# A decoder step on one core: one operand's passes on another engine, gate steps queued behind the weights, a prefilled pair of gate tiles, and a larger bank for the sample transposes

## The chip, the core and the metric

The kernel runs on one core of a Trainium2 chip. A core has a matrix engine (TensorE, PE in the profile, with its weight loads as PEld), a vector engine (VectorE, DVE), a scalar engine (ScalarE, ACT), GpSimd (POOL), and SyncE (SP), which here only issues DMA transfers. Each engine works through its own instructions in order. A waiting instruction therefore holds up everything behind it on that engine.

The metric is the device time of one launch, in microseconds (us). The kernel before takes 2475.88 us, the median of three runs from 2475.53 to 2476.44.

## The reference

One inference step of a layer is computed for a prompt of 512 tokens and for 8 samples of 4 tokens each, 544 tokens together. One wide projection feeds two branches, and a gated merge and a layer norm close the step:

```python
u = einsum('btd,dc->btc', x, w_in)          # D = 2048 -> 18952 columns
q_m,k_m,v_m,o_m,z_m, q_a,k_a,v_a,z_a, g_m,g_a, i_pre,f_pre = split(u)
ig, lf = i_pre + b_igate, log_sigmoid(f_pre + b_fgate)      # 4 heads each: "the gates"
h_m, C, n, m = mlstm(q_m, k_m, v_m, ig, lf, C0, n0, m0)     # 4 heads of 512, matrix memory
h_a = sliding_window_attention(q_a, k_a, v_a, sinks)        # 32 heads of 64, window 128
br_m = norm(h_m) * mlstm_norm_w * sigmoid(o_m) * silu(z_m)
br_a = h_a * silu(z_a)
y = sigmoid(g_m) * (br_m @ w_proj_m) + sigmoid(g_a) * (br_a @ w_proj_a)
out = layernorm(ALPHA * x + y @ w_out)
```

Everything is float32. The new states and the last key and value rows are returned too.

## The kernel before

**Precision.** A float32 operand is split in two float32r parts, a high part (a ScalarE cast) and the rest (a VectorE subtraction). A product is three matmuls: high by high, high by low and low by high. `split` (lines 194 to 203) does this to a 128x1024 tile of weights (`wh`, `wl`, two buffers each in pool `wp`), and `hilo` (243 to 245) to anything else.

**Start (lines 290 to 348).** x arrives in five transfers and is transposed on TensorE, 16 column blocks of 128, into PSUM tiles from `sm()`, a pool of four banks. The samples' 32 rows are transposed into one such tile, `pxs`, which lives until the last block. Each block goes through `hilo` into the operand tiles `a11`, `a21` (first half of the contraction) and `xk2` (second half). GpSimd rebuilds a float32 sum of high and low part (line 340) for `s1r` (from `a21`) and `n2r` (from `a11`), and adds them into `n3r` (line 348).

**Two plain products and the gates (lines 375 to 392 and 595 to 614).** The value columns of attention are computed by `gemm`, in two products of 128 columns, `kk` 0 and 1. Before each half of the second one `gates_half` multiplies the eight gate columns. Its weight tiles `wga`, `wgb` are taken from the `wh` and `wl` buffers, cleared by GpSimd (380, 381) and partly filled; the products go to two banks of the other PSUM pool, `bank()`.

**Paired products (lines 624 to 725).** All further columns are computed two blocks at a time by a scheme with seven block products in place of eight. Its x operands are prepared sums: `s1`, `n2`, `n3`, `s4`, made by the generator `x_sums` (553 to 585). `s4` is `n2r` subtracted from one part of `xk2`, plus the other part: GpSimd does both (577, 578), then `hilo` splits the result. The first pair needs `s4` at its sixth step. A pair has seven steps of 24 matmuls; `prepare` makes a step's weights (sums at line 646 or by an adding DMA at 644, then `split`) and is emitted up to three steps ahead with raised priority. Only two `wh`/`wl` buffers exist, so the cast for one step cannot begin before the step two places earlier has been multiplied. Raw weights come in four pieces, `b11`, `b12` (pool `wr`) and `b22`, `b21` (pool `wr2`, three buffers, which also hold the sum `t1` and, at the start, the samples' rows `xs`).

**Background work.** Generators are advanced by `tick` once per step. `gates` (395 to 521) turns the gate products into the decay tables. It computes `fg` (line 413), sends it through a small DMA to another layout (418), takes Abs and Exp on ScalarE (421, 422), a chain of short VectorE instructions (425 to 434), a DMA back (435), a scan (442), and so on.

**Order of instructions.** A planner orders each engine's instructions by priority and by when its own clock thinks that they are ready. `tc.issue_after(ins)` makes instructions of the same engine come after `ins` in that order. In `paired` all of `prepare`'s VectorE instructions are put after the last plain product's weight subtraction (`plain`, lines 702 and 709). `state["load"]` and `state["split"]` hold the latest weight load and the latest weight subtraction.

Of the kernel before, what the change touches and what calls it, by code (L numbers as in the profile page):

```python
# [16 lines left out]
F32R = mybir.dt.float32r  # L17
# [57 lines left out]
def _build(tc, nc, i, o, es):  # L75
# [25 lines left out]
    def nm(s):  # L101
        count[0] += 1
        return f"{s}_{count[0]}"

    def sm():
        return psB.tile([128, 512], F32, tag="sm", name=nm("sm"))
# [4 lines left out]
    def r32(ap):  # L111
        return ap.bitcast(F32)
# [81 lines left out]
    def split(raw, p=None, tags=("wh", "wl"), parts=1):  # L194
        p = p or wp
        wh = p.tile([128, 8, 128], F32R, tag=tags[0], name=nm("wh"))
        wl = p.tile([128, 8, 128], F32R, tag=tags[1], name=nm("wl"))
        n = 8 // parts
        for k in range(0, 8, n):
            A.copy(wh[:, k:k + n], raw[:, k:k + n])  # L200
            state["split"] = V.tensor_tensor(out=wl[:, k:k + n], in0=raw[:, k:k + n], in1=r32(wh[:, k:k + n]),  # L201
                                             op=ALU.subtract)
        return wh, wl
# [39 lines left out]
    def hilo(src, hi, lo, eng=None):  # L243
        A.copy(hi, src)
        (eng or V).tensor_tensor(out=lo, in0=src, in1=r32(hi), op=ALU.subtract)  # L245
# [41 lines left out]
    def two_k(ch):  # L287
        return slice(ch * 2, ch * 2 + 2)
# [23 lines left out]
    state["load"] = xdma  # L312
    with tc.issue_after(xdma.ins):
        raw0.append(load_half(win, VA_ + 128, 0))
    pxs = sm()
    for g in range(8):
        for q in range(2):
            k = g * 2 + q
            pt = sm()
            for t in range(4):  # L320
                PE.transpose(pt[:, t * 128:t * 128 + 128], xt[k][:, t], ident)
            if k == 2:
                for c in range(4):
                    PE.transpose(pxs[:, c * 128:c * 128 + 128], xs[:, c], ident)
            if k < 8:
                hilo(pt[:, 0:HT], a11[0][:, k], a11[1][:, k])
                hilo(pt[:, HT:SEQ], a21[0][:, k, 0:SEQ - HT], a21[1][:, k, 0:SEQ - HT])
            else:
                hilo(pt[:], xk2[0][k // 4 - 2][:, k % 4, 0:SEQ], xk2[1][k // 4 - 2][:, k % 4, 0:SEQ])
                c = (slice(None), k - 8, slice(0, SEQ - HT))  # L330
                state["x_end"] = V.tensor_tensor(out=s1r[c], in0=pt[:, HT:SEQ], in1=s1r[c], op=ALU.subtract)
        if g % 2:
            k4 = slice((g // 2) * 4, (g // 2) * 4 + 4)
            src = pxs[:].rearrange("p (c q t) -> p q c t", c=4, q=4)[:, g // 2]
            if g < 4:
                hilo(src, *(a21[p][:, k4, SEQ - HT:HT] for p in range(2)))
                for t_, (h_, l_) in ((s1r, a21), (n2r, a11)):
                    for ch in (g - 1, g):
                        ks_ = two_k(ch)
                        G.tensor_tensor(out=t_[:, ks_], in0=r32(h_[:, ks_]), in1=r32(l_[:, ks_]), op=ALU.add)  # L340
            else:
                hilo(src, *(xk2[p][g // 2 - 2][:, :, SEQ:T] for p in range(2)))
                c = (slice(None), slice(k4.start - 8, k4.stop - 8), slice(SEQ - HT, HT))
                V.tensor_tensor(out=s1r[c], in0=src, in1=s1r[c], op=ALU.subtract)
        if g == 3:
            for ch in range(4):
                ks_ = two_k(ch)
                G.tensor_tensor(out=n3r[:, ks_], in0=n2r[:, ks_], in1=s1r[:, ks_], op=ALU.add)
# [26 lines left out]
    def gates_half(ps, half):  # L375
        raw = wr.tile([128, 8, 128], F32, tag="raw", name=nm("graw"))
        nc.sync.dma_start(raw[:, :, 0:8], win[:, half * 8:half * 8 + 8, GI:GI + 8])
        wa = wp.tile([128, 8, 128], F32R, tag="wh", name=nm("wga"))
        wb = wp.tile([128, 8, 128], F32R, tag="wl", name=nm("wgb"))
        G.memset(r32(wa[:]), 0.0)  # L380
        G.memset(r32(wb[:]), 0.0)
        for g in range(2):
            src = raw[:, :, g * 4:g * 4 + 4]
            hi = wa[:, :, g * 32:g * 32 + 4]
            A.copy(hi, src)
            A.copy(wb[:, :, g * 32:g * 32 + 4], src)
            V.tensor_tensor(out=wa[:, :, 64 + g * 32:68 + g * 32], in0=src, in1=r32(hi), op=ALU.subtract)
        for kk in range(8):
            k = half * 8 + kk
            for n, (a, b) in enumerate(((wa, xh), (wb, xl))):  # L390
                for f, c, w in EVEN:
                    PE.matmul(ps[f][:, :w], a[:, kk], b(k, c, w),
                              start=(k == 0 and n == 0), stop=(k == 15 and n == 1))

    def gates(ps):
# [22 lines left out]
        nc.sync.dma_start(f7, fg)  # L418
        yield
        yield  # L420
        A.activation(e7, f7, AF.Abs)
        A.activation(e7, e7, AF.Exp, scale=-1.0)
        yield

        V.tensor_scalar(d7, e7, 2.0, None, op0=ALU.add)
        V.reciprocal(d7, d7)
        V.tensor_tensor(out=s7, in0=e7, in1=d7, op=ALU.mult)
        V.tensor_tensor(out=q7, in0=s7, in1=s7, op=ALU.mult)
# [7 lines left out]
        G.memset(rst, 1.0)  # L436
        G.memset(rst[:, 0:SEQ:128], 0.0)
        G.memset(rst[:, SEQ:T:NTS], 0.0)
        yield
        yield  # L440

        V.tensor_tensor_scan(c, rst, lf, 0.0, ALU.mult, ALU.add)
        ap = lf
        V.tensor_tensor(out=ap, in0=ig, in1=c, op=ALU.subtract)
        yield
# [107 lines left out]
    def x_sums():  # L553
        for ch in range(4):
            ks_ = two_k(ch)
            G.tensor_tensor(out=n2r[:, ks_], in0=n2r[:, ks_], in1=s1r[:, ks_], op=ALU.subtract)
            if ch % 2:
                yield
        for name, r_ in (("s1", s1r), ("n3", n3r), ("n2", n2r)):
            h_, l_ = S[name] = quad(act2, name)  # L560
            for ch in range(4):
                ks_ = two_k(ch)
                with tc.issue_after(state["x_end"].ins):
                    if name == "n3":
                        A.activation(h_[:, ks_], r_[:, ks_], AF.Copy, scale=-1.0)
                        V.scalar_tensor_tensor(l_[:, ks_], r_[:, ks_], -1.0, r32(h_[:, ks_]), op0=ALU.mult,
                                               op1=ALU.subtract)
                    else:
                        hilo(r_[:, ks_], h_[:, ks_], l_[:, ks_])
                if ch % 2:  # L570
                    yield

        for ch in range(4):
            ks_ = two_k(ch)
            k0 = (ch * 2) % 4
            h12, l12 = (r32(xk2[p][ch // 2][:, k0:k0 + 2, 0:HT]) for p in range(2))
            G.tensor_tensor(out=n2r[:, ks_], in0=h12, in1=n2r[:, ks_], op=ALU.subtract)
            G.tensor_tensor(out=n2r[:, ks_], in0=n2r[:, ks_], in1=l12, op=ALU.add)
        while not state.get("plain_done"):
            yield  # L580
        s4 = S["s4"] = quad(act, "s4")
        for ch in range(4):
            ks_ = two_k(ch)
            hilo(n2r[:, ks_], s4[0][:, ks_], s4[1][:, ks_])
            yield

# [109 lines left out]

    AHEAD = 400

    def paired(work):

        steps = [(w, n) for w in work for n in range(7)]
        ready, plain = 0, state["split"]
        with tc.issue_after(state["load"].ins):
            load_a(work[0])
            load_b(work[0])
        for at, (w, n) in enumerate(steps):

            while ready < min(at + 3, len(steps)):
                with tc.high_priority(offset=AHEAD), tc.issue_after(plain.ins):
                    prepare(*steps[ready])  # L710
                ready += 1
            p = at // 7 + 1
            if p < len(work):
                if n == 3:
                    load_a(work[p])
                elif n == 4:
                    load_b(work[p])
            if n == 2 and "early" in w:
                w["early"]()
            half_product(w, n)  # L720
            with tc.high_priority(offset=AHEAD):
                gather(w, n)
            if n == 6:
                w["end"](w["O1"], w["O2"])
            tick()
# [879 lines left out]
    def merge_pair(ct):  # L1605

        merges = []

        def early():
            merges.extend(merged(c) for c in (ct, ct + 1))  # L1610

        def end(o1, o2):
            for c, merge, o in zip((ct, ct + 1), merges, (o1, o2)):
                sg = merge([o[:, 0:HT], o[:, HT:T]])
                nc.sync.dma_start(d_y[c], sg[:])
        return dict(wv=wm, x=XM, cA=ct * 128, cB=ct * 128 + 128, scale=1.0, acc=True, end=end, early=early)

    paired([merge_pair(ct) for ct in range(4, 14, 2)])
    state["end"] = None
    esR.close()  # L1620
    tx = pool(esE, "ty", 6)
# [286 lines left out]
```

## Time and profile before

| | us |
|---|---|
| median of three runs | 2475.88 |
| profiled execution | 2477.29 |
| its span, first to last instruction | 2475.4 |
| TensorE busy | 2441.1 (99%) |
| VectorE busy | 1877.4 (76%) |
| ScalarE busy | 1215.2 (49%) |
| GpSimd busy | 531.7 (21%) |

The windows view gives the busy time of each engine in a stretch of the span, with the number of its instructions, the granted TensorE clock (PEclk, 1.00 is full), the busy share of the DMA engines and what they moved. A timeline row gives start, duration, engine, line, operation, output and inputs, shapes and count; in square brackets stand the idle time of the engine ahead of it and what ended it. `SPq` and `POOLq` rows are the issue of transfers. Starts are counted from the beginning of the span.

### The profile page before, as it was taken

Reading aid. Unit: us, or ns where it says so; the run is one execution under the profiler, and the core shown is the slowest. Engines: PE = TensorE matmul, PEld = TensorE weight load, DVE = VectorE, ACT = ScalarE, POOL = GpSimd, SP = SyncE. Lnnn points to the kernel's source line nnn. Section 1 sums busy time; section 2 is a strip of 40 time slices with the busy share of each in tenths; the row PEclk is TensorE's granted clock in tenths of the full one; section 3 lists DMA queues with packets and bytes.
Section 4 is the critical chain, followed back from the end, with each engine's and each line's share of the span. In section 5 each row is a group of like instructions: output and inputs, shape, how many; then the busy total and the mean of one; then the engine's idle time right before and its main releaser. Section 6 shows DMA issues by size and latency. Waiting matters only on the chain.

```text
span 2475.4 us, 48813 instructions
## 1 busy us (share of the span) xinstructions
PE 2441.1 (99%) x19446; PEld 2383.9 (96%) x19446; DVE 1877.4 (76%) x2805; ACT 1215.2 (49%) x1984; POOL 531.7 (21%) x492
## 2 busy tenths in 40 slices
PE   8999999999999999999999999999999999999997
PEld 8999999999999999999999999999999999999997
DVE  6768888888888887778877888887866654766667
ACT  4447667666667665443433444444633333344431
POOL 7113433433433431121011122111000000110111
PEclk9999999999999999999999999999999999999999
DMA  5676666676676655467678667587755546788776
GB/s 159 153 195 170 150 166 152 149 171 150 149 169 154 146 135 150 115 204 235 207 221 250 195 207 231 171 253 237 237 189 177 177 153 212 212 228 252 215 222 190
DMA packets 557435, 464.72 MB, mean 188 GB/s; under 512 B 45592, under 2 KB 454344, under 8 KB 556952
## 3 DMA queue, kind: packets, MB, share of 16 engines
q1 hardware_dynamic: 540312, 402.09, 54.6%
q0 software_dynamic: 15696, 57.15, 12.0%
q8 instruction: 153, 2.51, 0.4%
q10 hardware_dynamic: 1200, 2.36, 0.3%
q14 instruction: 74, 0.61, 0.1%
HBM read 319.06 MB, written 96.31 MB: 168 GB/s over the span
## 4 chain that ended last, share of the span: by engine, by line
PE 89%; DMA 4%; DVE 3%; POOL 1%; issue 1%; ACT 0%; SPq 0%; DVEq 0%; POOLq 0%; ACTq 0%
PE bank L666 45%; PE bank L668 22%; PE bank L210 10%; PE sm L1412 2%; PE bank L1224 1%; PE sm L1444 1%; PE sm L776 1%; PE sm L1457 1%; PE sm L822 1%; DMA tx<-d_y 1%; DMA ty<-d_y 1%; PE sm L1774 1%; DMA raw<-in_w_in 1%; DVE wl L201 1%; PE sm L802 1%
## 5 line engine op out<-in xcount | busy, mean ns | idle before, releaser
L200 ACT CAST wh<-raw 128x1024 fp32r<-128x1024 f32 x632 | 662.1, 1048 | 846.1 <-PE bank L666 682.8
L201 DVE TENSOR_TENSOR wl<-raw,wh 128x1024 fp32r<-128x1024 f32 x632 | 790.7, 1252 | 210.6 <-ACT wh L200 184.2
L666 PE MATMUL bank<-xk,wh 128*128 128x272 f32 x2336 | 322.7, 289 | 0.0
L646 DVE TENSOR_TENSOR raw<-raw,raw 128x1024 f32<-128x1024 f32 x238 | 303.5, 1276 | 7.6 <-DMA raw<-in_w_in 3.0
L666 PEld LDWEIGHTS bank<-xk,wh 128*128 128x128 f32 x2336 | 302.7, 188 | 3.5 <-issue 2.6
L685 POOL TENSOR_TENSOR ev<-p,ev 128x272 f32<-128x272 f32 x82 | 118.0, 1439 | 442.0 <-ACT ev L684 419.4
L666 PE MATMUL bank<-n2h,wh 128*128 128x272 f32 x656 | 171.2, 293 | 2.9 <-ACT wh L200 2.9
L666 PE MATMUL bank<-s1h,wh 128*128 128x272 f32 x656 | 169.8, 292 | 1.8 <-ACT wh L200 1.8
L666 PE MATMUL bank<-n3h,wh 128*128 128x272 f32 x656 | 169.4, 290 | 0.3 <-DVE ev L687 0.3
L668 PE MATMUL bank<-xk,wl 128*128 128x272 f32 x1168 | 169.6, 287 | 0.0
L666 PE MATMUL bank<-n2l,wh 128*128 128x272 f32 x656 | 169.2, 289 | 0.0
L666 PE MATMUL bank<-s1l,wh 128*128 128x272 f32 x656 | 168.0, 288 | 0.0
L666 PE MATMUL bank<-n3l,wh 128*128 128x272 f32 x656 | 167.7, 288 | 0.0
L666 PE MATMUL bank<-s4h,wh 128*128 128x272 f32 x656 | 167.1, 288 | 0.0
L666 PE MATMUL bank<-s4l,wh 128*128 128x272 f32 x656 | 166.8, 287 | 0.0
L668 PEld LDWEIGHTS bank<-xk,wl 128*128 128x128 f32 x1168 | 155.5, 188 | 0.0
L666 PE MATMUL bank<-a11h,wh 128*128 128x272 f32 x584 | 150.4, 289 | 0.3 <-ACT wh L200 0.3
L666 PE MATMUL bank<-a11l,wh 128*128 128x272 f32 x584 | 149.6, 288 | 0.0
L210 PE MATMUL bank<-bh,wl 128*128 128x272 f32 x704 | 148.3, 289 | 0.0
L210 PE MATMUL bank<-bh,wh 128*128 128x272 f32 x704 | 148.0, 289 | 0.0
L210 PE MATMUL bank<-bl,wh 128*128 128x272 f32 x704 | 146.0, 288 | 0.2 <-DVE bl L245 0.2
L644 POOL DMA_DIRECT2D raw<-raw x90 | 78.0, 867 | 277.2 <-DVE ev L693 202.2
(490 smaller groups left out, 5697.0 us busy)
## 6 DMA issues: line engine op xcount, KB each, us to landing
raw<-in_w_in SPq DMA_DIRECT2D x296, 512.0 KB
raw<-raw POOLq DMA_DIRECT2D x90, 512.0 KB, 4.9
C<-in_state_mlstm_C SPq DMA_DIRECT2D x32, 1024.0 KB
out<-C SPq DMA_DIRECT2D x64, 512.0 KB
raw<-in_w_proj_a SPq DMA_DIRECT2D x32, 512.0 KB
raw<-in_w_proj_m SPq DMA_DIRECT2D x32, 512.0 KB
raw<-in_w_out SPq DMA_DIRECT2D x32, 512.0 KB
d_v<-ev SPq DMA_DIRECT2D x16, 272.0 KB
```

The costliest lines, as they stand in the source:

```text
L200: A.copy(wh[:, k:k + n], raw[:, k:k + n])
L201: state["split"] = V.tensor_tensor(out=wl[:, k:k + n], in0=raw[:, k:k + n], in1=r32(wh[:, k:k + n]), op=ALU.subtract)
L210: PE.matmul(ps[f][:, :w], a[:, kk], b(k, c, w), start=(k == 0 and n == 0), stop=(k == 15 and n == 2))
L644: G.dma_start(out=w[out][:], in_=w[b][:], accum_op=ALU.add)
L646: V.tensor_tensor(out=w[out][:], in0=w[a][:], in1=w[b][:], op=ALU.add)
L666: PE.matmul(ps, wh[:, k], x(p, k), start=(first and k == 0 and p == 0), stop=False, skip_group_check=True)
L668: state["end"] = PE.matmul(ps, wl[:, k], x(0, k), start=False, stop=(k == 7), skip_group_check=True)
L685: G.tensor_tensor(out=c22, in0=p1, in1=c11, op=ALU.subtract)
L776: PE.matmul(pp[:, c0 + w0:c0 + 256], qs[a][:, j * 128:j * 128 + 128], kx[:, k0:k0 + 256 - w0], start=(n == 0), stop=(n == 1))
L802: PE.transpose(pt[:, b * 128:b * 128 + 128], s_[:, b, 128:256], ident)
L822: PE.matmul(po[:, b * 128:b * 128 + n], VA[:, b], p_[:, 2 * b:2 * b + n // 128], start=(b == 0 and m == 0), stop=(b == 3 and m == 1), skip ...
L1412: PE.matmul(pp[:, 0:258], a[:, b * 128:b * 128 + 128], b_[:, b, f], start=(b == 0 and n == 0), stop=(b == 3 and n == 2))
```

## The change

Five things are changed.

1. The two passes over `n2r` for `s4` are done by VectorE, not by GpSimd, and stand in the same loop as `s4`'s split, behind the end of the plain products.
2. `gates`' Abs is ordered behind the latest weight cast on ScalarE. Its VectorE chain and its scan are ordered behind the latest weight subtraction. The scan is emitted one tick later.
3. The gate weights have two tiles of their own, from pool `wr2`, cleared once by GpSimd at the start and used for both halves.
4. The samples are transposed into a tile of `bank()`, not of `sm()`.
5. `s1r` is copied from the transposes by ScalarE, eight copies of 240 columns and two of the samples' columns, in place of the GpSimd sums of `a21`. And `prepare` is ordered behind the plain subtraction only in the pairs of `w_proj_m`, not in those of `w_in` and `w_out`.

```diff
-            A.copy(wh[:, k:k + n], raw[:, k:k + n])
+            state["cast"] = A.copy(wh[:, k:k + n], raw[:, k:k + n])
...
-    pxs = sm()
+    gate_w = [wr2.tile([128, 8, 128], F32R, tag="raw2", name=nm("wg")) for _ in range(2)]
+    for t_ in gate_w:
+        G.memset(r32(t_[:]), 0.0)
+    pxs = bank()
...
                 hilo(pt[:, HT:SEQ], a21[0][:, k, 0:SEQ - HT], a21[1][:, k, 0:SEQ - HT])
+                A.copy(s1r[:, k, 0:SEQ - HT], pt[:, HT:SEQ])
...
-                for t_, (h_, l_) in ((s1r, a21), (n2r, a11)):
-                    for ch in (g - 1, g):
-                        ks_ = two_k(ch)
-                        G.tensor_tensor(out=t_[:, ks_], in0=r32(h_[:, ks_]), in1=r32(l_[:, ks_]), op=ALU.add)
+                A.copy(s1r[:, k4, SEQ - HT:HT], src)
+                for ch in (g - 1, g):
+                    ks_ = two_k(ch)
+                    G.tensor_tensor(out=n2r[:, ks_], in0=r32(a11[0][:, ks_]), in1=r32(a11[1][:, ks_]), op=ALU.add)
...
-        wa = wp.tile([128, 8, 128], F32R, tag="wh", name=nm("wga"))
-        wb = wp.tile([128, 8, 128], F32R, tag="wl", name=nm("wgb"))
-        G.memset(r32(wa[:]), 0.0)
-        G.memset(r32(wb[:]), 0.0)
+        wa, wb = gate_w
...
-        A.activation(e7, f7, AF.Abs)
+        with tc.issue_after(state["cast"].ins):
+            A.activation(e7, f7, AF.Abs)
...
-        V.tensor_scalar(d7, e7, 2.0, None, op0=ALU.add)
+        with tc.issue_after(state["split"].ins):
+            V.tensor_scalar(d7, e7, 2.0, None, op0=ALU.add)
...
-        yield
-        yield
-
-        V.tensor_tensor_scan(c, rst, lf, 0.0, ALU.mult, ALU.add)
+        for _ in range(3):
+            yield
+
+        with tc.issue_after(state["split"].ins):
+            V.tensor_tensor_scan(c, rst, lf, 0.0, ALU.mult, ALU.add)
...
+        while not state.get("plain_done"):
+            yield
+        s4 = S["s4"] = quad(act, "s4")
         for ch in range(4):
...
-            G.tensor_tensor(out=n2r[:, ks_], in0=h12, in1=n2r[:, ks_], op=ALU.subtract)
-            G.tensor_tensor(out=n2r[:, ks_], in0=n2r[:, ks_], in1=l12, op=ALU.add)
-        while not state.get("plain_done"):
-            yield
-        s4 = S["s4"] = quad(act, "s4")
-        for ch in range(4):
-            ks_ = two_k(ch)
+            V.tensor_tensor(out=n2r[:, ks_], in0=h12, in1=n2r[:, ks_], op=ALU.subtract)
+            V.tensor_tensor(out=n2r[:, ks_], in0=n2r[:, ks_], in1=l12, op=ALU.add)
             hilo(n2r[:, ks_], s4[0][:, ks_], s4[1][:, ks_])
...
-    def paired(work):
+    def paired(work, plain=None):
...
-        ready, plain = 0, state["split"]
+        ready = 0
...
-                with tc.high_priority(offset=AHEAD), tc.issue_after(plain.ins):
+                with tc.high_priority(offset=AHEAD), tc.issue_after(plain.ins) if plain else ExitStack():
                     prepare(*steps[ready])
...
-    paired([merge_pair(ct) for ct in range(4, 14, 2)])
+    paired([merge_pair(ct) for ct in range(4, 14, 2)], state["split"])
```

More of the change, by code (lines that the diff above doesn't have):

```diff
@@ L571, in x_sums @@
                     yield
-        for ch in range(4):
-            ks_ = two_k(ch)
[L575 to L578, printed above, removed]
         while not state.get("plain_done"):
@@ L583, in x_sums @@
             ks_ = two_k(ch)
+            k0 = (ch * 2) % 4
+            h12, l12 = (r32(xk2[p][ch // 2][:, k0:k0 + 2, 0:HT]) for p in range(2))
+            V.tensor_tensor(out=n2r[:, ks_], in0=h12, in1=n2r[:, ks_], op=ALU.subtract)
+            V.tensor_tensor(out=n2r[:, ks_], in0=n2r[:, ks_], in1=l12, op=ALU.add)
             hilo(n2r[:, ks_], s4[0][:, ks_], s4[1][:, ks_])
```

## The prediction

> **What bounds the kernel now.** I read the page's totals first, then the windows of 50 us over the whole span, then windows of 10 us over the start, and at last each engine's timeline there.
>
> ```profile
> span 2475.4 us, 48813 instructions
> PE 2441.1 (99%) x19446; PEld 2383.9 (96%) x19446; DVE 1877.4 (76%) x2805; ACT 1215.2 (49%) x1984; POOL 531.7 (21%) x492
> ```
>
> TensorE is idle for 2475.4 - 2441.1 = 34.3 us in all. No edit here removes a matmul of the products, so only idle time and slow-clock time can be won. The windows of the first 120 us show where they are.
>
> ```profile
> 0.00:10.00 10.00, 6.69 (x35) 6.70 (x36) 0.68 (x3) 2.25 (x5) 0.83 (x7) 1.00 0.84 238
> 10.00:20.00 10.00, 8.16 (x53) 7.70 (x52) 6.07 (x15) 6.02 (x17) 6.42 (x5) 0.83 1.09 358
> 20.00:30.00 10.00, 8.89 (x75) 8.70 (x74) 8.47 (x17) 6.62 (x17) 10.00 (x9) 1.00 0.36 34
> 30.00:40.00 10.00, 8.43 (x65) 7.85 (x63) 9.30 (x17) 5.81 (x14) 6.33 (x7) 1.00 0.59 154
> 40.00:50.00 10.00, 8.69 (x68) 8.34 (x68) 7.25 (x10) 5.02 (x12) 8.57 (x6) 1.00 0.55 146
> 50.00:60.00 10.00, 9.98 (x80) 9.77 (x80) 9.68 (x8) 4.47 (x9) 10.00 (x6) 1.00 0.20 54
> 60.00:70.00 10.00, 6.28 (x34) 5.73 (x33) 6.94 (x14) 4.88 (x10) 2.97 (x6) 0.69 0.47 106
> 70.00:80.00 10.00, 10.00 (x68) 9.99 (x68) 5.23 (x12) 3.48 (x5) 3.31 (x4) 0.80 0.49 108
> 80.00:90.00 10.00, 10.00 (x82) 10.00 (x82) 10.00 (x17) 3.16 (x3) 0.85 (x1) 1.00 0.63 173
> 90.00:100.00 10.00, 8.53 (x67) 7.97 (x66) 9.85 (x26) 6.28 (x11) 0.00 (x0) 1.00 0.58 144
> 110.00:120.00 10.00, 10.00 (x82) 10.00 (x81) 6.66 (x8) 4.35 (x6) 1.90 (x2) 1.00 0.78 190
> ```
>
> After the length of each stretch come PE, PEld, DVE, ACT and POOL, then the granted clock. The reader should see three things. An undisturbed 10 us hold 82 matmuls. The two windows from 60 to 80 hold 34 + 68 = 102 of 164, which is 62 / 8.2 = 7.6 us lost; 3.7 us of that are idle (10.00 - 6.28) and the other 3.9 us are the clock at 0.69 and 0.80. And VectorE is full from 80 to 100, where TensorE loses another 1.47 us.
>
> The waits of TensorE behind these numbers:
>
> ```profile
> 12.65 0.59 PE L210 MATMUL bank<-a21h,wh 128*128 128x272 f32 x1 [0.48 <-ACT a21h L244]
> 23.09 0.63 PE L321 MATMUL sm<-cc,xr 128*128 128x128 f32 x4 [1.11 <-DVE a21l L245]
> 33.71 0.37 PE L392 MATMUL bank<-a11h,wga 128*128 128x272 f32 x1 [1.19 <-DVE wga L387]
> 39.08 0.40 PE L210 MATMUL sm<-a11h,wh 128*128 128x272 f32 x1 [0.39 <-ACT wh L200]
> 40.74 0.44 PE L530 MATMUL sm<-cc,ev 128*128 128x128 f32 x2 [0.67 <-ACT ev L605]
> 41.93 0.39 PE L210 MATMUL sm<-a11h,wl 128*128 128x272 f32 x1 [0.64 <-DVE wl L201]
> 62.80 0.39 PE L666 MATMUL bank<-s1h,wh 128*128 128x272 f32 x1 [1.78 <-ACT wh L200]
> 67.96 0.59 PE L666 MATMUL bank<-n2h,wh 128*128 128x272 f32 x1 [1.94 <-ACT wh L200]
> 95.73 0.39 PE L666 MATMUL bank<-n2h,wh 128*128 128x272 f32 x1 [1.00 <-ACT wh L200]
> ```
>
> And ScalarE just before the two longest of them:
>
> ```profile
> 57.06 0.65 ACT L244 CAST s4h<-n2r 128x544 fp32r<-128x544 f32 x1 [2.98 <-POOL n2r L578]
> 61.16 0.64 ACT L244 CAST s4h<-n2r 128x544 fp32r<-128x544 f32 x1 [1.14 <-POOL n2r L578]
> 61.71 1.04 ACT L200 CAST wh<-raw 128x1024 fp32r<-128x1024 f32 x1
> 66.50 0.22 ACT L421 ACTIVATE t<-t 128x17 f32<-128x17 f32 x1 [3.06 <-DMA t<-t]
> 66.88 1.03 ACT L200 CAST wh<-raw 128x1024 fp32r<-128x1024 f32 x1
> ```
>
> The weight casts that TensorE waits for are not late by themselves. The one at 61.71 stands behind `s4h` casts that wait for GpSimd's passes, and the one at 66.88 behind the gates' Abs, which waits for the small DMA of `fg`. After 100 us the span holds few such waits, so what is won or lost at the start passes to the end.
>
> **The change part by part.**
>
> *The passes on VectorE and Abs behind a cast (60 to 80 us).* Both causes go. The passes leave GpSimd, so `s4h` waits for VectorE only. `s4`'s tiles take over those of `a21`, free when TensorE has finished the first half of the second plain product at 51.6, before the first pair. When Abs is emitted, two ticks into the first pair, the latest cast emitted is that of step 3, so Abs falls behind the casts of steps 2 and 3 (before, it stood ahead of step 2's). Then its DMA can be 3 us late without a matmul waiting. Queued behind it there are step 4's cast and ScalarE's copies out of PSUM. I take the whole 7.6 us as won; the low end is the 3.7 us of idle time alone, if the clock stays low for another reason.
>
> The price is on VectorE:
>
> ```profile
> 50.15 2.04 DVE L201 TENSOR_TENSOR wl<-raw,wh 128x1024 fp32r<-128x1024 f32 x1 [2.90 <-ACT wh L200]
> 52.12 2.38 DVE L646 TENSOR_TENSOR raw<-raw,raw 128x1024 f32<-128x1024 f32 x1
> 56.26 1.85 DVE L201 TENSOR_TENSOR wl<-raw,wh 128x1024 fp32r<-128x1024 f32 x1
> 58.03 1.88 DVE L245 TENSOR_TENSOR s4l<-n2r,s4h 128x544 fp32r<-128x544 f32 x1
> 61.66 0.71 DVE L245 TENSOR_TENSOR s4l<-n2r,s4h 128x544 fp32r<-128x544 f32 x1 [1.74 <-issue]
> 63.97 1.21 DVE L646 TENSOR_TENSOR raw<-raw,raw 128x1024 f32<-128x1024 f32 x1
> 65.11 1.21 DVE L201 TENSOR_TENSOR wl<-raw,wh 128x1024 fp32r<-128x1024 f32 x1
> L577 POOL TENSOR_TENSOR n2r<-xk,n2r x4: 1363/1860/3047, 45.4 to 53.4; 128x544 f32<-128x544 f32 x4
> ```
>
> Eight passes of 128x544 at 0.71 each are 5.7 us. Against that, the four VectorE instructions beside GpSimd's passes took 2.04 + 2.38 + 1.85 + 1.88 = 8.15, and the same shapes without them 1.21 + 1.21 + 1.21 + 0.71 = 4.34, so 3.8 us come back. Net 1.9 us more work. Its cover is VectorE's idle time from 40 to 80 us, 40 - (7.25 + 9.68 + 6.94 + 5.23) = 10.9 us. If TensorE runs some 8 us sooner, that cover shrinks by as much, and about 10.9 - 8 - 1.9 = 1 us is left before the stretch where VectorE is full. So it is nearly used up. I charge 1.0 us, the size of the wait that VectorE's queue already causes at 95.73; the ends are 0 and the 1.9 us of added work, and a gain of 1.0 if that wait itself goes.
>
> *Gate tiles of their own.* The waits at 39.08 and 41.93 come from the weight buffers: the gate tiles sat in them, so the second plain product's cast and subtraction started late. With buffers free the split can run before 39 us. I take 0.39 + 0.64 = 1.0 us; the wait of 0.67 at 40.74 belongs to copies on ScalarE and may go (high end) or stay. The two clears of 128x1024 move to the beginning, where POOL is busy for 0.83 of 10 us: nothing. The wait at 33.71 (1.19) I do not count. The second gate bank is now the one that `pxs` held, and that comes free only with the last reader:
>
> ```profile
> 35.50 0.28 DVE L344 TENSOR_TENSOR r<-sm,r 128x128 f32<-128x128 f32 x1
> 34.06 1.57 SPq L637 DMA_DIRECT2D raw<-in_w_in  x2
> 41.90 0.37 SPq L187 DMA_DIRECT2D raw<-in_w_in  x1
> ```
>
> GpSimd's earlier finish draws that reader forward, so the ends are a gain of 1.2 and a loss of 1.2.
>
> Another queue is touched. Before, `b22` and `b21` were requested at 34.06. Now two of the three `wr2` buffers hold gate tiles until the gates' last matmul, at about 49 us; `b21` and the sum `t1` wait for them. `b21` is first used three steps into the pair, some 9 us after the plain products end at 57.7, so a request at 49 is early enough: cost 0. If its request stands in SyncE's order ahead of `b11` (41.90), the first weights of the pair queue behind it; this is a rival below.
>
> *`pxs` in a bank and `s1r` from ScalarE (10 to 25 us).* A fourth transpose tile turns over, and GpSimd loses four sums. The wait at 23.09 came from a subtraction queued behind a weight subtraction that GpSimd's sum had stretched:
>
> ```profile
> 20.50 2.13 DVE L201 TENSOR_TENSOR wl<-raw,wh 128x1024 fp32r<-128x1024 f32 x1 [0.51 <-ACT wh L200]
> 11.78 0.36 ACT L244 CAST a21h<-sm 128x240 fp32r<-128x240 f32 x1
> ```
>
> I take the 1.1 us. ScalarE gets eight copies like the 0.36 one and two smaller, some 3.5 us, and has 20 - 6.02 - 6.62 = 7.4 us idle from 10 to 30. A late copy of this kind cost 0.48 at 12.65; I charge 0.5. Ends: 0 and 3.5.
>
> *The rest.* Gates' chain and scan behind splits, one tick later, and `prepare` without its order edge: the subtractions they are ordered against are ready before the other inputs in each case; cost 0, ends a microsecond either way.
>
> *Sum.* 7.6 - 1.0 + 1.0 + 1.1 - 0.5 = 8.2 us. The span becomes 2467.2 and the profiled execution, 1.9 us longer than its span, 2469.1. The median lies 1.4 us under the profiled execution, so 2475.88 - 8.2 = 2467.7.
>
> **The rivals.**
>
> *The clock stays low.* TensorE is idle for only 1.78 and 1.94 us before and in the slow stretch, while the 1.11 and 1.19 us at 23 and 34 are followed by full clock. If something other than these waits slows it, 3.9 us of the sum go: 2471.6. The timing speaks for the waits, because the clock is 1.00 in the window before them and falls after the first.
>
> [...]
>
> *A wait at the new buffers.* SyncE stands at `b21` from about 35 to 49 us, and `b11`, `b12` come some 7 us later than 41.90. TensorE then waits up to 4 us at the start of the first pair, and as at 62.80 the clock may follow (3.9): 2467.7 + 7.9 = 2475.6. For it: before, both loads were requested together at 34.06, ahead of `b11`. Against it: the planner orders a transfer by when its buffer comes free.
>
> *VectorE takes GpSimd's place (slower).* The gates' steps from 79 to 100 us share VectorE with the splits; busy time there is 19.85 of 20. A pair of steps later on that engine by the passes and with less cover would cost TensorE its waits in full. If the passes stand ahead of the splits, 5.7 us of them plus the four `s4l` at 0.71 (2.8) hold back weights, and the 3.9 us of slow clock follow: 12.4 lost where 8.2 and the 1.0 already charged are won, which gives 2479.1. It decides from a VectorE backlog of 5.3 us on (9.2 - 3.9). Against it: split instructions have raised priority, and passes can run before 51 us.
>
> *More is won.* The waits at 33.71, 40.74 and 95.73 go too (1.2 + 0.7 + 1.0), and the two charges (1.5) are not paid: 12.6 us, 2463.3.
>
> **How the numbers follow.** The forecast has 0.52, more won 0.18, the low clock 0.08, the new buffers 0.10, VectorE 0.12. 0.2% is 5 us, about what a measurement of this kernel can tell. Faster by more: 0.52 + 0.18 = 0.70. Within: 0.18 (low clock, buffers). Slower: 0.12. The range goes from 2462 (more won, and another microsecond from the order edges) to 2476 (the buffers' case), which leaves VectorE's case and little of the others outside.
>
> **What would show it.** Right: no `s4h` cast waiting for POOL, no weight cast behind Abs, a clock of 1.00 from 50 to 80 us, the second plain product's cast before 39 us, and the first pair starting 2 us sooner. Wrong: a new TensorE wait for a weight cast or subtraction in the first two pairs, SyncE waiting for TensorE at L637 with L187 behind it, or a clock under 1.00 somewhere between 15 and 80 us.

## The result, and the profile after

| | before | after |
|---|---|---|
| median of six runs, us | 2476.16 (2475.12 to 2478.39) | 2467.02 (2465.84 to 2469.53) |
| profiled execution, us | 2477.29 | 2469.53 |
| its span, us | 2475.4 | 2467.7 |

The ratio is 0.9963, with an interval from 0.995 to 0.9976: 9.1 us less. The page's totals of after:

```profile
span 2467.7 us, 48808 instructions
PE 2436.4 (99%) x19446; PEld 2379.8 (96%) x19446; DVE 1876.5 (76%) x2813; ACT 1216.6 (49%) x1994; POOL 509.8 (21%) x478
```

GpSimd's work falls by 22 us and VectorE's stays the same, although it took over eight passes. The windows of after, columns as before:

```profile
20.00:30.00 10.00, 6.59 (x51) 5.90 (x50) 6.04 (x14) 4.58 (x18) 5.06 (x4) 1.00 0.36 35
30.00:40.00 10.00, 10.00 (x82) 10.00 (x83) 9.70 (x15) 8.69 (x19) 5.78 (x4) 1.00 0.60 160
40.00:50.00 10.00, 10.00 (x82) 10.00 (x82) 10.00 (x18) 4.11 (x8) 0.00 (x0) 1.00 0.54 144
50.00:60.00 10.00, 10.00 (x84) 9.99 (x83) 10.00 (x14) 7.51 (x15) 1.27 (x2) 1.00 0.44 102
60.00:70.00 10.00, 10.00 (x83) 9.99 (x82) 8.91 (x23) 5.06 (x9) 4.17 (x5) 1.00 0.58 119
70.00:80.00 10.00, 10.00 (x82) 10.00 (x81) 7.67 (x12) 3.34 (x4) 1.91 (x3) 1.00 1.00 261
90.00:100.00 10.00, 8.86 (x71) 8.88 (x72) 9.62 (x21) 7.45 (x12) 0.40 (x1) 1.00 0.94 211
110.00:900.00 790.00, 790.00 (x6357) 789.81 (x6356) 647.08 (x951) 516.91 (x953) 273.79 (x210) 1.00 0.66 159
```

From 30 to 80 us TensorE is never idle in this profile, and always at full clock: the waits at 33.71, 39.08, 40.74, 41.93, 62.80 and 67.96 are all gone. But the window from 20 to 30 is worse than before, 6.59 busy where it was 8.89. The last row gives the rate to convert with: 6357 matmuls in 790 us, 8.05 per us.

TensorE's timeline of after shows what the bad window waits for, and the wait near 90:

```profile
25.49 0.40 PE L210 MATMUL bank<-xk,wh 128*128 128x272 f32 x1 [0.60 <-ACT xk L244]
29.89 0.52 PE L210 MATMUL bank<-xk,wh 128*128 128x272 f32 x2 [2.38 <-ACT xk L244]
91.14 0.37 PE L668 MATMUL bank<-n3h,wh 128*128 128x272 f32 x1 [1.32 <-DVE ev L689]
```

ScalarE's timeline of after, ahead of the wait of 2.38 us, and at the passes and Abs:

```profile
24.64 0.22 ACT L369 CAST sel<-cc 128x32 fp32r<-128x32 f32 x1 [2.00 <-DMA cc<-in_consts]
28.78 0.22 ACT L386 CAST wg<-graw 128x32 fp32r<-128x32 f32 x1 [3.12 <-DMA graw<-in_w_in]
29.26 0.57 ACT L244 CAST xk<-sm 128x512 fp32r<-128x512 f32 x1
...
53.04 1.28 ACT L244 CAST s4h<-n2r 128x544 fp32r<-128x544 f32 x2 [1.12 <-DVE n2r L585]
65.65 0.22 ACT L423 ACTIVATE t<-t 128x17 f32<-128x17 f32 x1 [0.79 <-DMA t<-t]
```

The `xk` cast that TensorE waits for at 29.89 stands in ScalarE's queue behind the copies into the gate tiles (lines 386, 387), and these wait 3.12 us for the raw gate columns to arrive. (The wait of 0.60 at 25.49 has another cause: its cast stands behind the copy of a constant, `sel`, that waits for `cc`.) Before, the gate tiles were weight buffers that came free later, so those copies were queued later. With tiles that are cleared at the start nothing else holds them back, and they moved ahead of the casts of x. SyncE's queue says why the columns are late:

```profile
18.94 5.43 SPq L365 DMA_DIRECT2D sinkb<-in_attn_sinks  x1
24.41 0.67 SPq L366 DMA_DIRECT2D sinkc<-in_attn_sinks  x1
25.20 1.13 SPq L381 DMA_DIRECT2D graw<-in_w_in  x2
```

The request of `graw` comes only after one that held the queue for 5.43 us.

**The same kernel before, profiled twice more.** The loss that the prediction was mostly made of, from 60 to 80 us, is not in these two profiles. The first of them:

```profile
30.00:40.00 10.00, 6.60 (x49) 5.78 (x47) 6.94 (x9) 5.61 (x14) 8.66 (x7) 0.93 0.60 161
40.00:50.00 10.00, 8.04 (x51) 8.05 (x52) 6.11 (x12) 3.00 (x7) 5.71 (x4) 0.72 0.54 139
60.00:70.00 10.00, 8.55 (x69) 8.34 (x68) 8.93 (x20) 4.81 (x10) 1.15 (x4) 1.00 0.49 106
```

```profile
41.95 0.60 PE L210 MATMUL sm<-a11h,wl 128*128 128x272 f32 x1 [4.30 <-DVE wl L201]
65.97 0.39 PE L666 MATMUL bank<-n2h,wh 128*128 128x272 f32 x1 [1.45 <-ACT wh L200]
```

```profile
35.86 4.91 DVE L566 SCALAR_TENSOR_TENSOR n3l<-r,n3h 128x544 fp32r<-128x544 f32 x4
40.69 1.21 DVE L201 TENSOR_TENSOR wl<-raw,wh 128x1024 fp32r<-128x1024 f32 x1
```

Here TensorE waits 4.30 us at 42, for the second plain product's weight subtraction. That one stands behind four `n3l` steps which took 4.91 us. And the clock is 0.72 around that wait, while it stays at 1.00 from 60 to 80. The span is the same within 1 us: 2475.5, and 2474.5 in the other. So the kernel before loses its time in one of two forms, and the prediction knew one. The form goes with the first 20 us. The two profiles of the first form (before, and only_passes below) start the first plain product at 11.65 and 12.08 us and have a clock of 0.83 from 10 to 20. The three of the second (with only_gate_order) start it at 10.85 to 11.01 and have 1.00. What makes that difference isn't shown.

**Where the time went, by stretches.** Matmuls that TensorE did in four stretches of the start, from the windows view of every profile (8.05 of them are 1 us; the last two columns are sums):

| kernel | 0 to 30 | 30 to 50 | 50 to 80 | 80 to 110 | 0 to 50 | 50 to 110 |
|---|---|---|---|---|---|---|
| before, as predicted from | 159 | 132 | 177 | 221 | 291 | 398 |
| before_again | 179 | 100 | 224 | 205 | 279 | 429 |
| before_third | 178 | 92 | 227 | 205 | 270 | 432 |
| after | 143 | 162 | 244 | 229 | 305 | 473 |
| after_again | 147 | 153 | 244 | 239 | 300 | 483 |
| undo_passes | 153 | 153 | 217 | 220 | 306 | 437 |
| undo_gate_order | 162 | 163 | 231 | 226 | 325 | 457 |
| undo_tiles | 172 | 125 | 237 | 232 | 297 | 469 |
| undo_start | 163 | 163 | 239 | 210 | 326 | 449 |
| only_passes | 159 | 132 | 219 | 218 | 291 | 437 |
| only_gate_order | 177 | 97 | 239 | 231 | 274 | 470 |
| gates_behind_x | 182 | 162 | 243 | 235 | 344 | 478 |
| sinks_later | 178 | 161 | 244 | 228 | 339 | 472 |

Means of three and two profiles: before 280 and 420, after 302.5 and 478. That is 22.5 / 8.05 = 2.8 us won before 50 us and 58 / 8.05 = 7.2 us behind it, 10 us together, and nearly all of it reaches the end: 9.1 us in the median. Of the 7.2 us, 4.3 lie from 50 to 80 (244 against a mean of 209.3) and 2.9 from 80 to 110 (234 against 210.3).

The first column also holds a difference that is not the kernels': the first plain product starts between 10.76 and 12.17 us, from one execution to the next (12.17 and 11.36 in the two of after).

### The profile page after: what moved, and what is told of

Its sections match the earlier page's. It is cut to its first block, busy times and chain, and to the rows that moved or that the text cites. A ratio compares the mean times of both kernels' runs of the same rounds, so it can differ in the third digit from the quotient of the medians.

```text
span 2467.7 us, 48808 instructions
## 1 busy us (share of the span) xinstructions
PE 2436.4 (99%) x19446; PEld 2379.8 (96%) x19446; DVE 1876.5 (76%) x2813; ACT 1216.6 (49%) x1994; POOL 509.8 (21%) x478
## 4 chain that ended last, share of the span: by engine, by line
PE 92%; DMA 3%; DVE 2%; SPq 1%; issue 1%; ACT 0%; DVEq 0%; POOL 0%; POOLq 0%
PE bank L668 45%; PE bank L670 22%; PE bank L210 10%; PE sm L1414 2%; PE bank L1226 1%; PE sm L1446 1%; PE sm L778 1%; PE sm L1459 1%; PE sm L824 1%; PE sm L210 1%; DMA tx<-d_y 1%; DMA ty<-d_y 1%; PE sm L1776 1%; DMA raw<-in_w_in 1%; PE sm L804 1%
```

## The experiments

**The passes back on GpSimd** (`undo_passes`), all else as in after:

```diff
+        for ch in range(4):
+            ...
+            G.tensor_tensor(out=n2r[:, ks_], in0=h12, in1=n2r[:, ks_], op=ALU.subtract)
+            G.tensor_tensor(out=n2r[:, ks_], in0=n2r[:, ks_], in1=l12, op=ALU.add)
         while not state.get("plain_done"):
             yield
...
-            V.tensor_tensor(out=n2r[:, ks_], in0=h12, in1=n2r[:, ks_], op=ALU.subtract)
-            V.tensor_tensor(out=n2r[:, ks_], in0=n2r[:, ks_], in1=l12, op=ALU.add)
```

> The changed kernel with only the two passes for the fourth operand back on GpSimd, in their old place. Theory (the prediction's first term): the weight cast of the first pair's second step stands again behind fourth-operand casts that wait for GpSimd; TensorE idles 1.5 to 2 us near 60 us, and the granted clock falls below 1.00 for some microseconds behind it. Loss against the changed kernel 1.8 (the wait alone) to 5.7 us (with 3.9 of slow clock): 2469 to 2473. Rival (the passes cost on VectorE what they save on ScalarE): within 1 us of the changed kernel, 2466 to 2468, and VectorE visibly less full from 40 to 60 us. On the clock: if waits cause the slow clock, PEclk is under 1.00 between 60 and 80 us; if it slows for another reason, that does not follow the wait.

Measured: 2474.51 us, ratio 0.999 [0.998, 0.9999]. That is 7.5 us over after, or 6.7 by the two ratios, and more than the expected 2469 to 2473. ScalarE's and TensorE's timelines:

```profile
53.04 0.65 ACT L244 CAST s4h<-n2r 128x544 fp32r<-128x544 f32 x1 [3.06 <-POOL n2r L582]
56.17 0.65 ACT L244 CAST s4h<-n2r 128x544 fp32r<-128x544 f32 x1 [2.48 <-POOL n2r L582]
58.48 0.65 ACT L244 CAST s4h<-n2r 128x544 fp32r<-128x544 f32 x1 [1.66 <-POOL n2r L582]
```

```profile
60.13 0.39 PE L670 MATMUL bank<-s1h,wh 128*128 128x272 f32 x1 [1.48 <-ACT wh L200]
```

The `s4h` casts wait for GpSimd again, and TensorE for a weight cast behind them. Up to 50 us the kernel stands where after stands (306 against 305 and 300); from 50 to 110 it is 41 matmuls short of the mean of after, 5.1 us. The clock, which was expected to fall behind the wait, is 1.00 from 50 to 80 us. The rest of the loss lies later. In this profile there are 5396 matmuls from 1700 to 2380 us, where after has 5418 and 5417; whether that is so in every execution isn't settled.

**The gates' order edges and the later tick taken out** (`undo_gate_order`):

```diff
-        with tc.issue_after(state["cast"].ins):
-            A.activation(e7, f7, AF.Abs)
+        A.activation(e7, f7, AF.Abs)
...
-        with tc.issue_after(state["split"].ins):
-            V.tensor_scalar(d7, e7, 2.0, None, op0=ALU.add)
+        V.tensor_scalar(d7, e7, 2.0, None, op0=ALU.add)
...
-        for _ in range(3):
-            yield
-        with tc.issue_after(state["split"].ins):
-            V.tensor_tensor_scan(c, rst, lf, 0.0, ALU.mult, ALU.add)
+        yield
+        yield
+        V.tensor_tensor_scan(c, rst, lf, 0.0, ALU.mult, ALU.add)
```

> The changed kernel without the order edges on the gates' Abs, VectorE chain and scan, and with the scan one tick sooner, as before. Theory: Abs stands ahead of a weight cast again and waits for its small transfer; TensorE idles up to 1.9 us near 65 us, alone or with a slow clock: 2468 to 2471. Rival (in the changed kernel that transfer is early enough, or Abs falls behind the casts anyway): no TensorE wait there, 2466 to 2468.

Measured: 2469.23 us, 0.9969 [0.9956, 0.9982], 2.2 us over after, with ranges that overlap. The total of matmuls up to 110 us is that of after, but it is made of two parts. The start went better, with a wait of 0.72 us at 27 and not of 2.38, though the edit changes nothing there: in this execution the first plain product started at 10.76 us, in after at 12.17, and the clock from 10 to 20 us was 0.83, not 1.00. From 50 to 110 it lacks 21 matmuls of after's mean, 2.6 us; 13 of them (1.6 us) lie before 80, and behind 80 the two profiles of after differ by 10 themselves. No wait is left near 65, where the prediction put Abs. There is a new one at 78.27, and VectorE's timeline shows what it waits behind:

```profile
78.27 1.27 PE L667 MATMUL bank<-a11h,wl 128*128 128x272 f32 x8 [1.32 <-DVE wl L201]
```

```profile
75.47 1.28 DVE L443 TENSOR_TENSOR_SCAN t<-t,t 4x544 f32<-4x544 f32 x1 [3.61 <-DMA t<-t]
76.68 0.40 DVE L692 SCALAR_TENSOR_TENSOR ev<-bank,ev 128x272 f32<-128x272 f32 x1
77.01 1.20 DVE L201 TENSOR_TENSOR wl<-raw,wh 128x1024 fp32r<-128x1024 f32 x1
```

VectorE stood 3.61 us at the scan, which waited for its small transfer, and the weight subtraction was queued behind it. In after that subtraction stands ahead of the scan, which waits for its transfer there too, but TensorE has no wait near it:

```profile
74.74 1.22 DVE L201 TENSOR_TENSOR wl<-raw,wh 128x1024 fp32r<-128x1024 f32 x1
77.31 1.28 DVE L446 TENSOR_TENSOR_SCAN t<-t,t 4x544 f32<-4x544 f32 x1 [1.35 <-DMA t<-t]
```

So with the passes moved it is the scan's place that pays, not that of Abs. Its edge and its later tick were taken out together, so which of the two is needed stays open.

**The gate tiles back in the weight buffers** (`undo_tiles`):

```diff
-    gate_w = [wr2.tile([128, 8, 128], F32R, tag="raw2", name=nm("wg")) for _ in range(2)]
-    for t_ in gate_w:
-        G.memset(r32(t_[:]), 0.0)
...
-        wa, wb = gate_w
+        wa = wp.tile([128, 8, 128], F32R, tag="wh", name=nm("wga"))
+        wb = wp.tile([128, 8, 128], F32R, tag="wl", name=nm("wgb"))
+        G.memset(r32(wa[:]), 0.0)
+        G.memset(r32(wb[:]), 0.0)
```

> The changed kernel with the gate tiles taken from the weight buffers and cleared for each half, as before. Theory: the second plain product's split waits for the gate products again, TensorE loses about 1 us around 40 us: 2468. Rival (the shared buffers delay the whole hand-over to the pairs, and with it casts near 50 to 60 us): 3 us or more and a wait there, 2470 or above. Second rival (the early gate copies on ScalarE, which in the changed kernel hold the transposes' casts until their transfer lands, near 29 us, go away with the late tiles): TensorE's wait of 2.4 us at 29.9 vanishes and the sum is even, 2465 to 2467.

Measured: 2469.42 us, 0.9969 [0.9957, 0.9982], 2.4 us over after, or 1.5 by the two ratios. The start gets better and the next stretch worse: from 20 to 30 us it does 70 matmuls where after does 51 and 48 (2.5 us), then from 30 to 50 it does 125 against 157.5 (4.0 us). The copies now stand behind more of the x casts. They still wait 1.29 us for `graw`, but TensorE's longest wait for an `xk` cast is 0.27 us, not 2.38. It waits again at 36 to 39, with a clock of 0.91 from 30 to 50:

```profile
38.47 0.44 PE L534 MATMUL sm<-cc,ev 128*128 128x128 f32 x2 [1.70 <-ACT ev L607]
```

So the tiles won 4.0 us and gave 2.5 back, 1.5 net.

**The start as before** (`undo_start`): `pxs` from `sm()`, `s1r` by GpSimd.

```diff
-    pxs = bank()
+    pxs = sm()
...
-                A.copy(s1r[:, k, 0:SEQ - HT], pt[:, HT:SEQ])
...
-                A.copy(s1r[:, k4, SEQ - HT:HT], src)
-                ... (n2r alone by GpSimd)
+                for t_, (h_, l_) in ((s1r, a21), (n2r, a11)):
+                    ...
```

> The changed kernel with the sample transposes in the smaller pool and the float sums of the second half-operand on GpSimd, as before. Theory (1.1 won less 0.5 charged): 2467.6, with the wait of about 1 us at 23 us back. Rival (ScalarE's ten copies are why the changed kernel loses 2.3 us more from 20 to 30 us): that loss goes, 2464 to 2466. Second rival (that loss comes from gate copies waiting for their transfer on ScalarE): the wait near 29 us stays in this kernel too.

Measured: 2469.98 us, 0.9971 [0.9959, 0.9982]. The wait for a transpose tile is back, and the wait for the x cast is shorter than in after, but still there:

```profile
20.69 0.63 PE L324 MATMUL sm<-cc,xr 128*128 128x128 f32 x4 [0.76 <-DVE a21l L245]
27.17 0.52 PE L210 MATMUL bank<-xk,wh 128*128 128x272 f32 x2 [1.40 <-ACT xk L244]
```

That part decides little by itself. Up to 50 us this kernel is ahead of after (326 against 302.5); from 80 to 110 it loses 24 matmuls (210 against 234) to weight casts and subtractions that come late. Why they do there was not pursued.

**The passes alone, in before** (`only_passes`): line 577 and 578 to VectorE, in the loop behind the plain products.

```diff
-            G.tensor_tensor(out=n2r[:, ks_], in0=h12, in1=n2r[:, ks_], op=ALU.subtract)
-            G.tensor_tensor(out=n2r[:, ks_], in0=n2r[:, ks_], in1=l12, op=ALU.add)
...
+            V.tensor_tensor(out=n2r[:, ks_], in0=h12, in1=n2r[:, ks_], op=ALU.subtract)
+            V.tensor_tensor(out=n2r[:, ks_], in0=n2r[:, ks_], in1=l12, op=ALU.add)
```

> The kernel before with only the two passes moved to VectorE. Theory as predicted (two separate causes, passes and Abs): the wait of 1.78 near 62 us goes, the one of 1.94 at Abs stays, and the slow clock stays or shrinks: 2 to 5 us faster than before, 2471 to 2474. Rival (the passes are the whole cause: with them gone the gates' first values and their transfer come early, and Abs no longer waits): both waits and the slow clock go, 7 us or more, 2469 or below. Second rival (without the gate tiles VectorE holds back weights): no gain.

Measured: 2474.35 us, 0.9993 [0.9984, 1.0002]: not clear of the noise, and 4 us at most, while undoing the same edit in after costs 7.5 us. The profile has before's first form, and does 39 matmuls more than that one from 50 to 110 us (437 against 398), so something is won there. VectorE's timeline, and TensorE's wait:

```profile
47.25 2.61 DVE L580 TENSOR_TENSOR n2r<-xk,n2r 128x544 f32<-128x544 f32 x4
49.80 2.61 DVE L581 TENSOR_TENSOR n2r<-n2r,xk 128x544 f32<-128x544 f32 x4
52.34 1.21 DVE L201 TENSOR_TENSOR wl<-raw,wh 128x1024 fp32r<-128x1024 f32 x1
```

```profile
53.60 0.52 PE L210 MATMUL sm<-xk,wl 128*128 128x272 f32 x2 [1.30 <-DVE wl L201]
```

The plain product's last weight subtraction stands behind all eight passes. This is the mechanism of the third rival, VectorE in GpSimd's place, at a price of 1.3 us. It does not act in after, where that subtraction is done by 44.9, before the passes begin:

```profile
43.67 1.21 DVE L201 TENSOR_TENSOR wl<-raw,wh 128x1024 fp32r<-128x1024 f32 x1
47.35 2.61 DVE L584 TENSOR_TENSOR n2r<-xk,n2r 128x544 f32<-128x544 f32 x4
```

Gate tiles of their own are not needed for that. In undo_tiles, without them, the subtraction stands behind all eight passes too, but the passes begin at 41.89 and not at 47.25, and TensorE does not wait for it:

```profile
41.89 0.70 DVE L584 TENSOR_TENSOR n2r<-xk,n2r 128x544 f32<-128x544 f32 x1
48.94 1.21 DVE L201 TENSOR_TENSOR wl<-raw,wh 128x1024 fp32r<-128x1024 f32 x1
```

And only_passes lacks the order edges: TensorE waits 1.01 us for VectorE at 79.10.

**The gates' order alone, in before** (`only_gate_order`): the same edit as undone above, put into before.

```diff
+            state["cast"] = A.copy(wh[:, k:k + n], raw[:, k:k + n])
...
+        with tc.issue_after(state["cast"].ins):
+            A.activation(e7, f7, AF.Abs)
...
```

> The kernel before with only the order edges on the gates' steps and the later scan. Theory as predicted: the wait of 1.94 us at Abs goes, the one at the fourth operand's casts (1.78) stays, and the slow clock stays or shrinks: 2 to 5 us faster, 2471 to 2474. Rival (Abs waits elsewhere, or the slow clock follows the first wait alone): under 1.5 us. If the clock is 1.00 from 60 to 80 us here, one wait of 1.8 us alone does not bring it down.

Measured: 2472.03 us, 0.9981 [0.9972, 0.999]. Its profile has before's second form, with a wait of 4.3 us for the weight subtraction at 40.89. Compared with the two profiles of that form it has as many matmuls up to 50 us (274) and 38 to 41 more from there to 110, 4.9 us. Of these, 12 to 15 lie before 80: at 65.13 it waits 0.24 us where before_again waits 1.45 behind Abs. The other 26 lie from 80 to 110. There this run has no wait of TensorE for VectorE near 80, where before_again has one of 1.02 us at 81.27 and before_third one of 1.00 at 81.81. So while the passes are still on GpSimd, the order is worth more than beside the passes' move.

**After, once more** (`after_again`), with nothing changed.

> The changed kernel once more, as the yardstick for the runs beside it. 9 us under the kernel before (ratio 0.9963). If the loss of 2.6 us in the last 70 us of its first profile was of that execution alone, the span here is 2 to 3 us shorter than 2467.7; if it belongs to the program, it is there again.

Measured: 2466.66 us, 0.996 [0.9948, 0.9973]; the span of the profile is 2465.1 us, 2.6 less than in the first, as was expected if the first lost something of its own near its end. The waits of 0.61 and 2.37 us on `xk` casts are there again, at 24.70 and 29.09, so they are no accident of one profile. Behind the second the clock is low this time:

```profile
30.00:40.00 10.00, 10.00 (x73) 10.00 (x72) 9.65 (x15) 7.37 (x17) 5.74 (x4) 0.86 0.60 158
```

**The gate copies behind the casts of x** (`gates_behind_x`): after, with an order edge on what waits for `graw` and the constants.

```diff
+                state["x_cast"] = state["hi"]   # the last x cast
...
+    with tc.issue_after(state["x_cast"].ins):
+        A.copy(sel[:], cc[:, C_SEL:C_SEL + 32])
...
+            with tc.issue_after(state["x_cast"].ins):
+                A.copy(hi, src)
+                A.copy(wb[:, :, g * 32:g * 32 + 4], src)
+            with tc.issue_after(state["x_end"].ins):
+                V.tensor_tensor(out=wa[:, :, 64 + g * 32:68 + g * 32], in0=src, in1=r32(hi), op=ALU.subtract)
```

> The changed kernel with the copies of the gate weights (and two small constants) ordered behind the last transposes' cast on ScalarE, and their subtraction behind the last such instruction on VectorE. Theory (the changed kernel's wait of 2.4 us at 29.9 comes from these copies, which wait for the gate weights' transfer while casts of transposes stand behind them): the waits of 2.38 and 0.60 us go, 2 to 3 us faster than the changed kernel, 2464 to 2465. Rival (the waiting only moves, to the gate products or to the split of the second plain product): within 1 us of the changed kernel.

Measured: 2462.23 us (2460.74 to 2463.18), 0.9939 [0.9926, 0.9951]. It beats both kernels, after by 4.4 us (after_again ran beside it). Windows and ScalarE's timeline:

```profile
20.00:30.00 10.00, 9.58 (x80) 9.34 (x79) 10.00 (x22) 8.34 (x23) 7.74 (x6) 1.00 0.43 48
```

```profile
27.76 0.59 ACT L244 CAST xk<-sm 128x512 fp32r<-128x512 f32 x1 [0.56 <-PE sm L324]
28.25 0.22 ACT L390 CAST wg<-graw 128x32 fp32r<-128x32 f32 x1
```

The copies now stand behind the last x cast and wait for nothing, and 41.5 matmuls more than after's mean are done by 50 us, 5.2 us; 8 of them lie before 20 us, in the part that differs between executions. The order of these copies was the cause.

**The sinks' transfers requested later** (`sinks_later`): the copies stay where after has them, but `graw` is requested earlier.

```diff
-        nc.sync.dma_start(sinkb[:], i["attn_sinks"].partition_broadcast(128))
-        nc.sync.dma_start(sinkc[:], i["attn_sinks"].unsqueeze(1).to_broadcast([AH, NTS]))
...
+    with tc.issue_after(state["load"].ins):
+        (both, ahead of state["plain_done"] = True)
```

> The changed kernel with the two small transfers of the attention sinks (whose issue occupies SyncE for 5.4 us ahead of the gate weights' transfers) requested later. Theory (ScalarE's gate copies wait for the gate weights' transfer, and the transposes' casts behind them): the transfer lands some 5 us sooner, the wait of 2.4 us of TensorE near 29 us goes, 2463 to 2465. Rival (the copies' place in the order matters, not the transfer): the wait stays, within 1 us of the changed kernel.

Measured: 2464.59 us (2462.82 to 2465.84), 0.9945 [0.9928, 0.9961]. The wait of 2.38 is gone, 0.32 of the first remains. SyncE's queue:

```profile
17.68 5.71 SPq L379 DMA_DIRECT2D graw<-in_w_in  x2
25.82 0.65 SPq L614 DMA_DIRECT2D sinkb<-in_attn_sinks  x1
```

The cause is confirmed from its other end: the copies harm because their data is late.

**Before, twice more** (`before_again`, `before_third`), with nothing changed.

> The kernel before, profiled again. If the slow clock from 63 to 73 us belongs to the two waits of 1.8 and 1.9 us ahead of it, both are there again with a clock under 1.00 in the windows from 60 to 80 us, and about 102 matmuls in them. If the clock falls by chance of its own, the waits are there and the clock is 1.00 (near 130 matmuls), or it falls elsewhere.

> The same once more, for how much of the slow clock returns: 102 matmuls from 60 to 80 us if it follows the waits each time, between 102 and 133 if only sometimes.

Measured: 2477.36 and 2476.39 us. Both profiles have the second form shown above (100 and 92 matmuls from 30 to 50, clock 0.72 and 0.66 from 40 to 50).

The order edge of `prepare` was not undone by itself, so its share is open. The four parts that were undone cost 7.5, 2.2, 2.4 and 3.0 us over after, 15.1 together for a gain of 9.1: they overlap, so none of these is a share of the gain.

## Why the prediction was right, and where it was not

The time was 2467.02 us where 2467.7 was predicted, but errors cancelled in it in two places: between the stretches behind 50 us, and within the gate tiles. That the sum came out so near is luck.

*Passes and Abs, 7.6 us, less 1.0.* Together they are 6.6, and 7.2 us were won from 50 to 110, but not where the prediction put them. The 7.6 belong to 60 to 80 us. Against the one profile that they were read from, 8.3 us were won from 50 to 80; against the mean of the three, 4.3, because in the other form the kernel before loses that time ahead of 50. The other 2.9 come from 80 to 110, where the prediction had a charge. The causes held in part. The passes on GpSimd are one (undone, 5.1 us go from 50 to 110). But the loss at 68, put to Abs, needs no edge once the passes are off GpSimd: in undo_gate_order and in only_passes, both without the edges, nothing waits there. What the edges pay is the scan at 77, where the prediction priced them at nothing ("cost 0"): 1.3 us at that wait, 1.6 us from 50 to 80.

*The low clock (first rival).* It fell: the clock is 1.00 from 50 to 80. That the waits of 1.78 and 1.94 had slowed it isn't shown: no other run has the two together, and undo_passes keeps 1.00 behind a wait of 1.48. Nor does the length of a wait decide it in these runs: 4.30 us in before_again and 4.3 in only_gate_order stand with a clock of 0.72 and 0.67 from 40 to 50, and 1.78 and 1.94 in before with 0.69 from 60 to 70; a wait of 2.37 in after_again was followed by 0.86, one of 2.38 in after by 1.00.

*The VectorE charge of 1.0.* Not paid. TensorE did 229 and 239 matmuls from 80 to 110, before 221, 205 and 205. Its wait there is 1.32 us in one profile of after and 0.17 in the other, where the first profile of before had 1.00 at 95.73. The end below nothing was the right one, and too small: 2.9 us on the mean. Which edit wins them isn't singled out: from 80 to 110, only_gate_order does 231 with the passes still on GpSimd, only_passes 218 and undo_gate_order 226.

*Gate tiles, 1.0 us.* This is the step that failed, in both directions. "I take 0.39 + 0.64 = 1.0 us" sized it by one profile; in the other form of before the same subtraction cost 4.30 us and the clock after it, and undoing the tiles loses 4.0 us from 30 to 50. And "the two clears of 128x1024 move to the beginning: nothing" counted GpSimd's time alone. The clears made the tiles ready early, the planner put their copies ahead of the x casts on ScalarE, and there they waited for `graw`, which made TensorE wait 2.38 us; no rival named that wait. By undo_tiles the stretch from 20 to 30 loses 2.5 us by it. The net, 1.5 us, is near the 1.0 only because the two errors have opposite signs.

*`pxs` and `s1r`, 1.1 less 0.5.* The wait for the tile is gone and comes back when undone, at 0.76. Its worth at the end can't be read off: what undo_start loses lies at 80 to 110.

*The other rivals.* The new buffers fell: `b21` is requested at 47.45, and no wait follows.

```profile
47.45 0.37 SPq L639 DMA_DIRECT2D raw<-in_w_in  x1
```

VectorE in GpSimd's place did not happen in after; in only_passes its order of instructions does, at 1.3 us and without the slow clock. More won was within reach: gates_behind_x is at 2462.23, where that rival gave 2463.3, by a wait that the rival did not know.

## What to carry to other kernels

Giving a tile its own buffer also takes away the wait that kept its fills late: look at which queue the fills stand in, what data they need, and order them behind the work that is urgent there. An edit's worth depends on the others: the passes alone bring nothing clear of the noise here, and with any two of the three other parts that were undone the kernel is 7.0 to 7.7 us faster than before. One profile shows one form of a start; profile twice before sizing a wait.

## What the runs showed of the hardware

- The same kernel, before, did 102 matmuls from 60 to 80 us in one execution, and 148 and 154 in two others, which did 100 and 92 from 30 to 50 where the first did 132. The spans agree within 1 us.
- Four `n3l` steps on VectorE took 4.91 us from 35.86 while two GpSimd passes ran beside them (before_again, the first line), and 2.62 us without (first profile of before, the second):

```profile
35.78 3.13 POOL L556 TENSOR_TENSOR n2r<-n2r,r 128x544 f32<-128x544 f32 x2
36.97 2.62 DVE L566 SCALAR_TENSOR_TENSOR n3l<-r,n3h 128x544 fp32r<-128x544 f32 x4
```

Why the steps take longer beside the passes isn't shown.
- In before, after, undo_gate_order, gates_behind_x and sinks_later one request on SyncE's queue is held until 21.4 to 24.4 us, whichever it is: `sinkb` for 5.43 us from 18.94 in after, `graw` for 5.71 from 17.68 in sinks_later, where `sinkb` at 25.82 took 0.65. What holds it isn't shown.
- A wait of 2.37 us was followed by a clock of 0.86 in one execution of after, and one of 2.38 by 1.00 in another.
